# Where a hybrid decoder layer normalises its rows: chunk 0 after the projection instead of before it, chunks 2 and 3 squared ahead of time

## The chip, the cores and the metric

The kernel runs on one core of a Trainium2 chip. The metric is the time of one execution on the device in microseconds (us). TensorE is written PE below, its weight loads PEld, VectorE DVE, ScalarE ACT, GpSimd POOL; SP is SyncE, whose queue issues nearly all transfers.

## The reference

One decoder layer on x of 2048 rows by 1024 columns, float32:

```
hn   = rms_norm(x, g_pre)                 # row * 1/rms(row) * g_pre
proj = hn @ w_in                          # 1024 -> 4096, cut into eight groups of 512
y_rg = rg_lru(conv4(rg_x)) * silu(rg_g)   # gated linear recurrence, 8 heads of 64
y_da = norm((softmax(q1 k1) - lam * softmax(q2 k2)) v) * (1 - l0) * silu(da_g)  # causal, 4 heads
y_xa = softmax(xa_q km) vm * silu(xa_g)   # 4 heads on 256 memory rows, km and vm from rms_norm(mem, g_mem)
out  = x + rms_norm(concat(y_rg, y_da, y_xa) @ w_out, g_post)
```

A row's 1/rms is one number per token, so `(x * r * g) @ w` equals `((x * g) @ w) * r`.

## The kernel before, in words

Each float32 matmul is three float32r matmuls on high and low halves: `mm3` adds hi*hi, lo*hi and hi*lo (L241). A weight piece of 128 by 512 is loaded by `w_load` into one of three raw buffers, and `w_conv` (L327) splits it: ACT casts the high half, POOL or DVE subtracts the low half. The split weights are also stored to memory (`WD`) and loaded back in the second half of the kernel.

Tokens are worked in four chunks of 512. Chunks 0 and 1 go through all 16 pairs of output blocks first, then chunks 2 and 3 in the order `ORDER_B`, then the output projection runs over 16 tiles of 128 rows. A pair has four steps `u`: two chunks by two halves, and a step is 24 matmuls of 512 columns into one of two PSUM banks (`psM`). The evictions `ev_qk`, `ev_v`, `ev_g`, `ev_xa` and `ev_rg` then read the bank.

To feed a chunk, its rows are normalised, transposed on PE in 128 by 128 blocks, scaled by g_pre and split into `hnT` (`transpose_norm`, L293). Chunk 0's rows go through `norm_row` (L264): one half is squared on ACT, one on DVE, a chain of small operations gives 1/rms, and both halves are scaled in place (L275). Chunks 1 to 3 and mem go through `norm_steps` (L277): a square on ACT every `gap` of planned time, then the chain, then all scales at once. In `woven` (L384) the transposes of a chunk stand between the first pair's matmuls, block by block (`kb`).

The order of PE's instructions is that of the program. A planner, `now`, adds up PE's expected time; `spawn` adds a generator that `pump` advances when its due time has come, between matmuls. So attention is woven into the projections: `s_stream` emits the scores (S) of a job, `t_stream` the transposed probabilities times V, `kv_stream` loads keys and values. `room["e"]` counts free score tiles of the pool `pe` (`N_E` = 12), and `kready` and `q2s` hold the planned arrival of keys and the loaded q tiles. A job is a head and a pair of 128-row query blocks. Twelve jobs can be done while chunks 0 and 1 are projected; `next_x` (L919), called at pair 13, waits in the plan for these twelve, then loads the rows of chunks 2 and 3 and spawns their `norm_steps`.

All other engines' queues are ordered by the framework by priority, which is program order unless `high_priority` moves it ahead, and by when its own plan sees operands and buffers ready. So a load can be issued well before its place in the program. Each buffer pool is a set of equal slots (`p2` nine, `p4` seven, `pw` six, `pe` twelve).

Of the kernel before, what the change touches and what calls it, by code (L numbers as in the profile page):

```python
# [57 lines left out]
def hybrid_layer(  # L58
# [66 lines left out]
    ones_r = const.tile([128, 128], F32R, name="ones_r")  # L125
# [16 lines left out]
    def setup():  # L142

        nc.scalar.preload_act_table_set("natural_log_exp_and_others")
        nc.scalar.dma_start(vec, vecs[:, 0:V_CW])
        make_identity(nc, ident)
        nc.gpsimd.memset(cmask, 0.0)
        nc.gpsimd.affine_select(
            out=cmask, in_=cmask, pattern=[[-1, 128]], compare_op=ALU.is_ge,
            fill=NEG, base=0, channel_multiplier=1)  # L150
        nc.vector.memset(epsb, EPS)
        nc.vector.memset(tinyb, 1e-37)
        nc.vector.tensor_scalar(ones_r, ident, 0.0, 1.0, op0=ALU.mult, op1=ALU.add)
# [110 lines left out]
    def norm_row(row):  # L264

        ss = tiny.tile([128, 2], F32, tag="ss1", name="ss1")
        ja, jv = f2("junk", (128, 512)), f2("junk", (128, 512))
        nc.scalar.activation(ja, row[0], AF.Square, accum_out=ss[:, 0:1])
        nc.vector.tensor_tensor_reduce(jv, row[1], row[1], 1.0, 0.0, ALU.mult, ALU.add, ss[:, 1:2])
        r = tiny.tile([128, 1], F32, tag="rs1", name="rs1")  # L270
        with tc.high_priority(offset=2000):
            nc.vector.tensor_add(r, ss[:, 0:1], ss[:, 1:2])
            rsqrt_mean(r, r, D, nc.vector)
            for p in row:
                nc.vector.tensor_scalar_mul(p, p, r)  # L275
# [93 lines left out]
    stored = set()  # L369
    setup()  # L370
# [12 lines left out]

    def woven(c, rows):  # L384

        new_hnT(c)
        os = [ps_m("ip") for _ in range(2)]
        xt = transpose_norm(rows, hnT[c], V_GPRE)
        next(xt)
        next(xt)  # L390
        for kb in range(KB):
            w = wcv[kb // 2]
            for half in range(2):
                cs = slice(half * 128, half * 128 + 128)
# [12 lines left out]
        ready.add(c)  # L407
        return os

# [61 lines left out]

    def ev_qk(h, c, which, o):
        t = f4("qkhl", (128, 2, CH), F32R)
# [16 lines left out]
    def ev_v(hp, c, half, o):  # L490
# [3 lines left out]
        for hh in range(2):  # L494
            nc.scalar.copy(t[:, 0, hh], ov[:, hh])
            nc.vector.tensor_sub(t[:, 1, hh], ov[:, hh], asf(t[:, 0, hh]))
# [5 lines left out]
    def ev_g(hp, c, half, o):  # L502
        t = f2("gs", (128, CH))
# [14 lines left out]
    def ev_xa(h, c, which, o):  # L518
        if which == 0:
# [63 lines left out]
    def ev_rg(b, c, which, o):  # L583
        if which == 0:
# [7 lines left out]
            nc.scalar.copy(xr[:, 3:515], o)  # L592
# [14 lines left out]
        xc, xh = state.pop("xc")  # L607
        gs = f2("rgg", (128, CH))
# [5 lines left out]
    def rg_gates(b, c, xc, xh, gs):  # L614
# [83 lines left out]
    def s_stream(jobs):  # L698

        q2s = {}  # L700

        def q2_load(i):
            if i < 2 * len(jobs) and i not in q2s:
                h, pr = jobs[i // 2]
                if has("qk", h, pr // 4):
                    q2s[i] = load_q2(h, 2 * pr + i % 2)
        due = now[0]
        for ij, (h, pr) in enumerate(jobs):
# [3 lines left out]
            while kready.get((h, pr // 4), 1e9) > now[0]:  # L712
# [119 lines left out]
    def subln(h, pr, A, B):  # L832
        c, j = divmod(pr, 2)
        s = ps_t("ss", (128, 256))
        mm(s, ones_r, B[:, 0, :], True, False)
        mm(s, ones_r, B[:, 1, :], False, True)
# [72 lines left out]
    def start_attention():  # L909
        room["e"] = N_E  # L910
# [6 lines left out]
    xn = {}  # L917

    def next_x():  # L919
# [19 lines left out]
    def start_b():  # L939
# [5 lines left out]
        (2, 0): start_attention,  # L945
        (13, 0): next_x,
# [12 lines left out]

    def load_wout(grp):  # L960
# [6 lines left out]
        for kb in range(4):  # L967
            raw = f4("woraw")
            nc.sync.dma_start(raw, w_out[4 * grp + kb])
# [9 lines left out]
    project((2, 3), 80, ORDER_B, {(0, 0): start_b, (15, 2): last_pair})  # L979
# [118 lines left out]
```

## Time and profile before

| | before |
|---|---|
| time, median of 3 runs | 1467.82 us (1467.02 to 1468.22) |
| the profiled execution | 1467.53 us, span 1465.7 us |
| PE busy, and its mean granted clock | 1412.3 us (96%), 0.994 of full speed |
| DVE, ACT, POOL busy | 898.3, 775.9, 477.3 us |
| transfers | 234.37 MB, mean 160 GB/s |

The span runs from the first to the last instruction. Busy times overlap; an engine's idle time counts only where the chain that sets the end passes through it. PE's matmuls are pipelined, so their busy time can cover short stalls.

### The profile page before, as it was taken

To read this page: it belongs to the slowest core of one execution; us is meant where nothing else is said; L and a number is where in the kernel's file an instruction comes from. 1 tells how busy PE (TensorE), PEld (TensorE's weight loads), DVE (VectorE), ACT (ScalarE), POOL (GpSimd) and SP (SyncE) were. 2 spreads that over 40 slices of the span, in tenths; PEclk is the share of its full clock that TensorE was granted. 3 is DMA by queue.
4 is the path that set the end of the run, shared out by engine and by line. 5 is a ranking of instruction groups with operands and counts; after the bars stand their busy time and mean duration, and the time that the engine had idled before them with its cause. 6 is when DMAs were issued, how large, how long until landed. Compare 5 with 4: busy or idle time off the path is not lost.

```text
span 1465.7 us, 21854 instructions
## 1 busy us (share of the span) xinstructions
PE 1412.3 (96%) x7568; PEld 1199.2 (82%) x7568; DVE 898.3 (61%) x1872; ACT 775.9 (53%) x1900; POOL 477.3 (33%) x568
## 2 busy tenths in 40 slices
PE   5999999999999899999999999999999999999997
PEld 3798889888887678888887898888877888888886
DVE  6531555676644876746547666757678777767222
ACT  6343544666547784745555545555566545554221
POOL 2031333344435632412213222212255333334221
PEclk9999999999999999999999999999999999999999
DMA  8689787745433348356324554232475334322231
GB/s 298 180 263 338 230 240 237 247 143 181 166 119 110 134 163 247 121 173 196 114 97 118 165 177 168 86 113 70 143 251 169 101 135 150 102 76 94 87 122 72
DMA packets 147870, 234.37 MB, mean 160 GB/s; under 512 B 12464, under 2 KB 82224, under 8 KB 147760
## 3 DMA queue, kind: packets, MB, share of 16 engines
q1 hardware_dynamic: 147616, 232.98, 48.8%
q8 instruction: 59, 0.97, 0.3%
q14 instruction: 51, 0.42, 0.1%
q10 hardware_dynamic: 144, 0.01, 0.0%
HBM read 142.76 MB, written 90.18 MB: 159 GB/s over the span
## 4 chain that ended last, share of the span: by engine, by line
PE 73%; DVE 9%; ACT 7%; DMA 4%; POOL 3%; issue 3%; SPq 1%; DVEq 0%; POOLq 0%; ACTq 0%
PE ip L198 36%; PE po L198 16%; PE s L198 7%; PE o L198 6%; PE pt L202 3%; PE xas L198 2%; DVE e L766 1%; DVE nm L740 1%; PE xao L198 1%; DMA q<-QD 1%; DVE xc L600 1%; PE rgo L198 1%; ACT e L742 1%; PE xat L202 1%; POOL e L765 1%
## 5 line engine op out<-in xcount | busy, mean ns | idle before, releaser
L198 PE MATMUL ip<-hnT,wp 128*128 128x512 f32 x2688 | 680.5, 397 | 6.9 <-DVE rgg L610 2.6
L198 PEld LDWEIGHTS ip<-hnT,wp 128*128 128x128 f32 x2688 | 496.0, 190 | 109.8 <-DVE hnT L307 4.5
L742 ACT ACTIVATE e<-s,nm 128x512 f32<-128x512 f32 (+3 forms) x320 | 200.1, 626 | 254.7 <-DVE nm L740 235.8
L740 DVE TENSOR_REDUCE nm<-s 128x1 f32<-128x512 f32 (+3 forms) x320 | 193.4, 605 | 37.4 <-PE s L198 33.1
L198 PE MATMUL po<-wout,yg 128*128 128x512 f32 x768 | 193.4, 393 | 5.0 <-POOL wout L239 2.4
L765 POOL TENSOR_SCALAR e<-e,f 128x512 f32<-128x512 f32 (+3 forms) x160 | 121.3, 773 | 235.5 <-DVE f L761 161.6
L198 PE MATMUL s<-kv,q 128*128 128x512 f32 (+3 forms) x640 | 182.9, 367 | 3.9 <-DMA q<-QD 2.4
L198 PEld LDWEIGHTS po<-wout,yg 128*128 128x128 f32 x768 | 141.1, 188 | 35.4 <-POOL wout L239 4.2
L766 DVE SCALAR_TENSOR_TENSOR e<-e,f 128x512 f32<-128x512 f32 (+3 forms) x160 | 138.0, 887 | 29.9 <-POOL e L765 29.7
L807 DVE TENSOR_TENSOR pthl<-pt,pthl 128x512 fp32r<-128x512 f32 (+1 forms) x144 | 94.5, 656 | 68.0 <-ACT pthl L806 67.5
L198 PE MATMUL o<-pthl,kv 128*128 128x256 f32 (+1 forms) x864 | 134.3, 290 | 1.0 <-DVE pthl L807 0.9
L198 PEld LDWEIGHTS s<-kv,q 128*128 128x128 f32 x640 | 114.5, 189 | 25.1 <-DMA q<-QD 3.0
L239 POOL TENSOR_TENSOR wp<-wraw,wp 128x512 fp32r<-128x512 f32 x67 | 91.1, 1368 | 127.1 <-ACT wp L238 110.8
L198 PEld LDWEIGHTS o<-pthl,kv 128*128 128x128 f32 x864 | 114.1, 189 | 4.5 <-DVE pthl L807 1.8
L806 ACT CAST pthl<-pt 128x512 fp32r<-128x512 f32 (+1 forms) x144 | 80.7, 561 | 55.2 <-PE pt L202 54.5
L239 POOL TENSOR_TENSOR yg<-yraw,yg 128x512 fp32r<-128x512 f32 x48 | 64.2, 1341 | 132.8 <-ACT yg L238 122.4
L198 PE MATMUL ip<-wp,hnT 128*128 128x256 f32 x768 | 99.7, 284 | 1.3 <-POOL wp L239 0.8
L198 PEld LDWEIGHTS ip<-wp,hnT 128*128 128x128 f32 x768 | 95.8, 191 | 3.0 <-POOL wp L239 1.0
L198 PE MATMUL po<-wo,yg 128*128 128x512 f32 x384 | 97.2, 392 | 0.0
L202 PE MATMUL pt<-ident,e 128*128 128x128 f32 x544 | 83.0, 272 | 3.3 <-DVE pthl L807 3.3
L198 PEld LDWEIGHTS po<-wo,yg 128*128 128x128 f32 x384 | 71.0, 188 | 14.3
L202 PEld LDWEIGHTS pt<-ident,e 128*128 128x128 f32 x544 | 66.9, 140 | 18.4 <-DVE pthl L807 3.8
(188 smaller groups left out, 1686.1 us busy)
## 6 DMA issues: line engine op xcount, KB each, us to landing
WD<-wp SPq DMA_DIRECT2D x64, 512.0 KB, 4.7
wp<-WD SPq DMA_DIRECT2D x64, 512.0 KB, 4.3
wraw<-in_w_in_dram SPq DMA_DIRECT2D x64, 256.0 KB, 3.4
q<-QD SPq DMA_DIRECT2D x128, 128.0 KB, 3.7
kv<-KD SPq DMA_DIRECT2D x24, 512.0 KB, 5.9
kv<-VD SPq DMA_DIRECT2D x24, 512.0 KB, 6.2
yraw<-YD SPq DMA_DIRECT2D x48, 256.0 KB, 2.7
QD<-qkhl SPq DMA_DIRECT2D x32, 256.0 KB, 3.5
```

Of the source, the lines that this page charges most:

```text
L198: nc.tensor.matmul(o, w, xx, start=start, stop=stop)
L202: nc.tensor.transpose(o, i, ident)
L239: eng.tensor_sub(lo, raw, asf(hi))
L600: nc.vector.scalar_tensor_tensor(xc[:, 0:CH], xr[:, k:k + CH], vec2[:, cw + k:cw + k + 1], xc[:, 0:CH], op0=ALU.mult, op1=ALU.add)
L740: nc.vector.tensor_reduce(out=nm[:, c, kc:kc + 1], in_=s[:, 0:w], op=ALU.max, axis=AX.X, negate=True)
L742: nc.scalar.activation(e[kc, c][:, 0:w], s[:, 0:w], AF.Exp, bias=nm[:, c, kc:kc + 1], accum_out=l[:, c, kc:kc + 1])
L765: nc.gpsimd.tensor_scalar(e2, e2, f[:, 1, kc:kc + 1], 1.0, op0=ALU.mult, op1=ALU.mult)
L766: nc.vector.scalar_tensor_tensor(e1, e1, f[:, 0, kc:kc + 1], e2, op0=ALU.mult, op1=ALU.add)
L806: nc.scalar.copy(hi[:, 0:n], t[:, 0:n])
L807: nc.vector.tensor_sub(lo[:, 0:n], t[:, 0:n], asf(hi[:, 0:n]))
```

## The change

Chunk 0 is no longer normalised before it is transposed. `norm_row` is gone; `inv_rms`, called in `woven` after block 2, squares chunk 0's eight half-tiles (four on ACT, four on DVE) and leaves 1/rms in `r0`, one column per 128 rows. `spread` transposes each column, broadcast to 128 by 128, on PE, so that every partition of `rB0` holds the 512 numbers, and keeps `rB0` in a `pe` slot. Every result of chunk 0 is multiplied by `rB0` when it leaves PSUM (`normed_out`), and V, whose tokens lie on partitions, by `r0`'s column. x's first halves are loaded before its second halves, with weights 1 and 2 after each; chunk 1 is loaded at block 3, mem after the woven pair. Weight 0 is split on DVE, the other first weights on POOL.

`ahead`, spawned at step (4, 0), loads the rows of chunks 2 and 3 half a tile at a time into one `pe` slot and squares them in place on ACT. `next_x` loads the rows again and spawns `scale_rows`, which scales half a row every `SQ_GAP`. The plan has 11 score tiles, 10 while `ahead` runs.

Besides: `ones_r` is one column that is broadcast; in `rg_gates` the two matmuls on the low half stand behind the four on the high half; `s_stream` waits until 6 planned us after the load of a job's first q tile; the raw rows of w_out's group 2 are asked for at step (15, 3) of the second half.

```diff
-    ones_r = const.tile([128, 128], F32R, name="ones_r")
+    ones_r = const.tile([128, 1], F32R, name="ones_r")
...
-    def norm_row(row):
...
+    def inv_rms(tiles, r):
+        n = len(tiles)
+        ss = tiny.tile([128, 2, n], F32, tag="ss0", name="ss0")
+        for j in range(2):
+            for i, row in enumerate(tiles):
+                junk = f2("junk", (128, 512))
+                if i % 2:
+                    nc.vector.tensor_tensor_reduce(junk, row[j], row[j], 1.0, 0.0, ALU.mult, ALU.add,
+                                                   ss[:, j, i:i + 1])
+                else:
+                    nc.scalar.activation(junk, row[j], AF.Square, accum_out=ss[:, j, i:i + 1])
+        nc.vector.tensor_add(r, ss[:, 0], ss[:, 1])
+        rsqrt_mean(r, r, D, nc.vector)
...
     w_load(0)
-    xr0 = load_rows(x, 4, "xrow")
-    w_load(1, 2)
+    xr0 = [[f2("xrow", (128, 512), pool=pe) for _ in range(2)] for _ in range(4)]
+    for j in range(2):
+        for i in range(4):
+            nc.sync.dma_start(xr0[i][j], x[i * 128:(i + 1) * 128, j * 512:(j + 1) * 512])
+        w_load(1 + j)
+    rB0 = f2("rB0", (128, CH), pool=pe)
     xb = bigt("xrows", (128, 4, 2, 512), F32)
...
-    for i in range(4):
-        nc.sync.dma_start(xb[:, i].rearrange("p a b -> p (a b)"), x[CH + i * 128:CH + (i + 1) * 128, :])
-    mrows = load_rows(mem, 2, "memx")
-    w_conv(0)
-    for row in xr0:
-        norm_row(row)
-    w_conv(1, 2, eng=nc.vector)
+    mrows = []
+    with tc.high_priority(offset=2000):
+        w_conv(0, eng=nc.vector)
+    w_conv(1, 2)
...
             if c == 0:
+                if kb == 2:
+                    with tc.high_priority(offset=1000):
+                        inv_rms(rows, r0)
+                if kb == 6:
+                    spread(r0, 4, rB0)
+                if kb == 3:
+                    for i in range(4):
+                        t0 = CH + i * 128
+                        nc.sync.dma_start(xb[:, i].rearrange("p a b -> p (a b)"), x[t0:t0 + 128, :])
                 if kb in (1, 2, 4, 6):
                     i = {1: 3, 2: 4, 4: 5, 6: 6}[kb]
-                    w_conv(i, eng=nc.vector if i in (3, 5) else nc.gpsimd, pool=pw if i < 6 else p4)
+                    w_conv(i, pool=pw if i < 6 else p4)
...
             w_conv(7, pool=p4)
+            mrows.extend(load_rows(mem, 2, "memx"))
...
+    def spread(r, n, dst):
+        t = ps_t("rb", (128, n * 128))
+        for i in range(n):
+            transpose(t[:, i * 128:(i + 1) * 128], r[:, i:i + 1].to_broadcast([128, 128]))
+        with tc.high_priority(offset=2000):
+            nc.scalar.copy(dst, t)
...
+    def normed_out(o, c):
+        if c:
+            return o
+        n = f2("nrm", (128, CH))
+        nc.vector.tensor_mul(n, o, rB0)
+        return n
...
+        o = normed_out(o, c)
...
+                r = r0[:, 2 * half + i:2 * half + i + 1]
+                nc.scalar.activation(hi, oi, AF.Copy, scale=r)
+                nc.vector.scalar_tensor_tensor(lo, oi, r, asf(hi), op0=ALU.mult, op1=ALU.subtract)
...
-            nc.scalar.copy(xr[:, 3:515], o)
+            if c == 0:
+                nc.vector.tensor_mul(xr[:, 3:515], o, rB0)
+            else:
+                nc.scalar.copy(xr[:, 3:515], o)
...
+        os = [ps_s("rgo") for _ in range(2)]
         for g in range(2):
-            o = ps_s("rgo")
-            mm3(o, state["rgh"][:, b, g, :], state["rgl"][:, b, g, :], xh[:, 0], xh[:, 1], True, True)
+            mm(os[g], state["rgh"][:, b, g, :], xh[:, 0], True, False)
+            mm(os[g], state["rgl"][:, b, g, :], xh[:, 0], False, False)
+        for g in range(2):
+            o = os[g]
+            mm(o, state["rgh"][:, b, g, :], xh[:, 1], False, True)
...
                     q2s[i] = load_q2(h, 2 * pr + i % 2)
+                    landed[i] = now[0] + 6.0
...
-            while kready.get((h, pr // 4), 1e9) > now[0]:
+            while max(kready.get((h, pr // 4), 1e9), landed[2 * ij]) > now[0]:
                 yield 0.5
...
-        room["e"] = N_E
+        room["e"] = N_E - 1
...
+    def ahead():
+        ssx = const.tile([128, 8, 2], F32, name="ssx")
+        while room["e"] < 1:
+            yield 0.4
+        room["e"] -= 1
+        for k in range(16):
+            row = f2("xahead", (128, 512), pool=pe)
+            t0, j = 2 * CH + (k // 2) * 128, k % 2
+            nc.sync.dma_start(row, x[t0:t0 + 128, j * 512:j * 512 + 512])
+            yield 9.0
+            nc.scalar.activation(row, row, AF.Square, accum_out=ssx[:, k // 2, j:j + 1])
+            yield 4.0
+        room["e"] += 1
+        nc.gpsimd.tensor_add(rx, ssx[:, :, 0], ssx[:, :, 1])
+        rsqrt_mean(rx, rx, D)
+
+    def scale_rows(c):
+        for i, row in enumerate(xn[c]):
+            for p in row:
+                nc.vector.tensor_scalar_mul(p, p, rx[:, 4 * (c - 2) + i:4 * (c - 2) + i + 1])
+                yield SQ_GAP
...
-            spawn(norm_steps(xn[c], SQ_GAP), 6.0 if c == 2 else 20.0)
+            spawn(scale_rows(c), 6.0 if c == 2 else 20.0)
...
-            room["e"] += 8
+            room["e"] += 9
...
+        (4, 0): lambda: spawn(ahead()),
...
+    def last_raw():
+        for kb in range(4):
+            wo_load(2, kb)
...
-    project((2, 3), 80, ORDER_B, {(0, 0): start_b, (15, 2): last_pair})
+    project((2, 3), 80, ORDER_B, {(0, 0): start_b, (15, 2): last_pair, (15, 3): last_raw})
```

## Rows read from the trace of the kernel before

**Rows 1.** The page, busy us (share of the span) and instructions of each engine.
```profile
PE 1412.3 (96%) x7568; PEld 1199.2 (82%) x7568; DVE 898.3 (61%) x1872; ACT 775.9 (53%) x1900; POOL 477.3 (33%) x568
```

**Rows 2.** TensorE's waits: line, what for, us in total, times, longest us.
```profile
PE xt L202 <- DVE xrow L275: 14.3, 4, 9.4
...
PE rgo L198 <- POOL xchl L604: 4.0, 5, 1.4
...
PE xas L198 <- DVE xaq L528: 3.4, 3, 1.7
...
PE ip L198 <- DVE rgg L610: 2.6, 2, 1.4
...
PE po L198 <- POOL wout L239: 2.4, 4, 0.7
...
PE s L198 <- DMA q<-QD: 2.4, 1, 2.4
...
PE po L198 <- ACT wout L238: 1.5, 1, 1.5
...
PE ip L198 <- DVE qkhl L476: 1.4, 2, 0.7
```

**Rows 3.** Timeline of the start: start us, busy us, instruction [idle before <-releaser].
```profile
7.39 0.69 DVE L269 CUSTOM_DVE_ANT_0 junk<-xrow 128x512 f32<-128x512 f32 x1
...
15.15 0.88 DVE L275 TENSOR_SCALAR xrow<-xrow,rs 128x512 f32<-128x512 f32 x2
...
16.95 2.93 PE L198 MATMUL ip<-hnT,wp 128*128 128x512 f32 x6
...
47.08 1.03 PE L202 MATMUL xt<-ident,xrows 128*128 128x128 f32 x8
...
50.33 0.60 PE L202 MATMUL xt<-ident,xrows 128*128 128x128 f32 x4
```

**Rows 4.** Windows: us, busy (x) PE PEld DVE ACT POOL, PEclk, DMA share, GB/s.
```profile
480.00:490.00 10.00, 8.08 (x27) 6.19 (x28) 9.58 (x13) 9.44 (x22) 5.04 (x6) 0.83 0.57 205
...
510.00:520.00 10.00, 8.84 (x32) 7.12 (x33) 5.70 (x6) 7.33 (x13) 4.24 (x6) 0.83 0.49 159
```

**Rows 5.** Timeline of the RG-LRU stretch.
```profile
457.28 0.62 ACT L283 ACTIVATE junk<-xrow 128x512 f32<-128x512 f32 x1
...
479.43 7.38 DVE L291 TENSOR_SCALAR xrow<-xrow,rs 128x512 f32<-128x512 f32 x8 [0.94 <-POOL rs L256]
...
480.67 0.73 PE L198 MATMUL rgo<-xchl,rgh 128*128 128x512 f32 x2 [1.40 <-POOL xchl L604]
...
487.45 8.45 PE L198 MATMUL ip<-hnT,wp 128*128 128x512 f32 x36 [1.25 <-DVE rgg L610]
...
511.16 0.73 PE L198 MATMUL rgo<-xchl,rgh 128*128 128x512 f32 x2 [1.16 <-POOL xchl L604]
```

**Rows 6.** Timeline around attention's first scores.
```profile
136.71 1.62 SPq L692 DMA_DIRECT2D q<-QD  x2
...
145.65 0.81 PE L198 MATMUL s<-kv,q 128*128 128x256 f32 x2 [2.38 <-DMA q<-QD]
...
146.30 4.05 PE L198 MATMUL ip<-hnT,wp 128*128 128x512 f32 x10
```

**Rows 7.** Groups: busy us, mean ns of one | idle before, releaser.
```profile
L239 POOL TENSOR_TENSOR wp<-wraw,wp 128x512 fp32r<-128x512 f32 x67 | 91.1, 1368 | 127.1 <-ACT wp L238 110.8 <-DMA kv<-VD 15.9
...
L505 DVE TENSOR_TENSOR gs<-ip,gs 128x512 f32<-128x512 f32 x16 | 11.0, 689 | 27.3 <-ACT gs L262 27.0
```

**Rows 8.** ScalarE's waits, one row.
```profile
ACT wp L238 <- DMA wraw<-in_w_in_dram: 13.9, 11, 2.5
```

**Rows 9.** Timeline: end of attention's first part, and w_out.
```profile
413.71 0.40 PE L198 MATMUL ss<-sq,ones_r 128*128 128x256 f32 x2
...
1083.92 10.68 SPq L969 DMA_DIRECT2D woraw<-in_w_out_dram  x5
...
1092.35 0.73 PE L198 MATMUL po<-wout,yg 128*128 128x512 f32 x2 [1.52 <-ACT wout L238]
```

More of the change, by code (lines that the diff above doesn't have):

```diff
@@ L152, in setup @@
         nc.vector.memset(tinyb, 1e-37)
-        nc.vector.tensor_scalar(ones_r, ident, 0.0, 1.0, op0=ALU.mult, op1=ALU.add)
+        nc.vector.tensor_scalar(ones_r, ident[:, 0:1], 0.0, 1.0, op0=ALU.mult, op1=ALU.add)
     def setup2():
@@ L262, in sigmoid @@
         nc.scalar.activation(o, o, AF.Exp, scale=-1.0)
-    def norm_row(row):
[L266 to L275, printed above, removed]
+    def inv_rms(tiles, r):
[11 more added lines that the diff above has]
+        rsqrt_mean(r, r, D, nc.vector)
     def norm_steps(tiles, gap, eng=nc.gpsimd, prio=2000):
@@ L369, in hybrid_layer @@
     stored = set()
+    r0 = const.tile([128, 4], F32, name="r0")
     setup()
     w_load(0)
-    xr0 = load_rows(x, 4, "xrow")
-    w_load(1, 2)
+    xr0 = [[f2("xrow", (128, 512), pool=pe) for _ in range(2)] for _ in range(4)]
[4 more added lines that the diff above has]
+    rB0 = f2("rB0", (128, CH), pool=pe)
     xb = bigt("xrows", (128, 4, 2, 512), F32)
     xr1 = [[xb[:, i, j, :] for j in range(2)] for i in range(4)]
-    for i in range(4):
-        nc.sync.dma_start(xb[:, i].rearrange("p a b -> p (a b)"), x[CH + i * 128:CH + (i + 1) * 128, :])
-    mrows = load_rows(mem, 2, "memx")
-    w_conv(0)
-    for row in xr0:
-        norm_row(row)
-    w_conv(1, 2, eng=nc.vector)
+    mrows = []
+    with tc.high_priority(offset=2000):
+        w_conv(0, eng=nc.vector)
+    w_conv(1, 2)
     def woven(c, rows):
@@ L493, in ev_v @@
         ov = o.rearrange("p (t h d) -> p h t d", t=2, h=2)
-        for hh in range(2):
-            nc.scalar.copy(t[:, 0, hh], ov[:, hh])
-            nc.vector.tensor_sub(t[:, 1, hh], ov[:, hh], asf(t[:, 0, hh]))
+        for i in range(2):
+            if c:
+                hi, lo, oi = t[:, 0, i], t[:, 1, i], ov[:, i]
+                nc.scalar.copy(hi, oi)
+                nc.vector.tensor_sub(lo, oi, asf(hi))
+            else:
+                hi, lo, oi = t[:, 0, :, i], t[:, 1, :, i], ov[:, :, i]
+                r = r0[:, 2 * half + i:2 * half + i + 1]
+                nc.scalar.activation(hi, oi, AF.Copy, scale=r)
+                nc.vector.scalar_tensor_tensor(lo, oi, r, asf(hi), op0=ALU.mult, op1=ALU.subtract)
         def st():
@@ L502, in ev_g @@
     def ev_g(hp, c, half, o):
+        o = normed_out(o, c)
         t = f2("gs", (128, CH))
@@ L518, in ev_xa @@
     def ev_xa(h, c, which, o):
+        o = normed_out(o, c)
         if which == 0:
@@ L591, in ev_rg @@
                 nc.gpsimd.tensor_copy(xr[:, 0:3], halo[:, b, :])
-            nc.scalar.copy(xr[:, 3:515], o)
+            if c == 0:
+                nc.vector.tensor_mul(xr[:, 3:515], o, rB0)
+            else:
+                nc.scalar.copy(xr[:, 3:515], o)
             if c < NCH - 1:
@@ L607, in ev_rg @@
         xc, xh = state.pop("xc")
+        o = normed_out(o, c)
         gs = f2("rgg", (128, CH))
@@ L698, in s_stream @@
     def s_stream(jobs):
-        q2s = {}
+        q2s, landed = {}, {}
         def q2_load(i):
@@ L834, in subln @@
         s = ps_t("ss", (128, 256))
-        mm(s, ones_r, B[:, 0, :], True, False)
-        mm(s, ones_r, B[:, 1, :], False, True)
+        ones = ones_r.to_broadcast([128, 128])
+        mm(s, ones, B[:, 0, :], True, False)
+        mm(s, ones, B[:, 1, :], False, True)
         r = A[:, 1, :]
@@ L917, in hybrid_layer @@
     xn = {}
+    rx = const.tile([128, 8], F32, name="rx")
+    def ahead():
[18 more added lines that the diff above has]
+                yield SQ_GAP
     def next_x():
@@ L957, in y_granule, with wo_load @@
         return g
+    woraw = {}
+    def wo_load(grp, kb):
+        if (grp, kb) not in woraw:
+            raw = woraw[grp, kb] = f4("woraw", pool=pw if grp == 2 and kb == 3 else p4)
+            nc.sync.dma_start(raw, w_out[4 * grp + kb])
+        return woraw[grp, kb]
     def load_wout(grp):
@@ L967, in load_wout @@
         for kb in range(4):
-            raw = f4("woraw")
-            nc.sync.dma_start(raw, w_out[4 * grp + kb])
+            raw = wo_load(grp, kb)
             for j in range(2):
```

## The prediction

> **What bounds the kernel now.** I read the page's busy line first, then TensorE's waits, then the start and the stretches that the waits point at. TensorE has a matmul in flight 96% of the span, and no engine but its own weight loads passes 61% [rows 1]. Busy time of pipelined matmuls flatters the engine, so I don't look for time inside it: what can be won is its idle time, 1465.7 - 1412.3 = 53.4 us, and what is lost while its clock is granted below full speed. The largest part of the idle time lies before the first projection matmul at 16.95: TensorE waited 14.3 us for scaled rows of x [rows 2, 3]. The last few us follow the last matmul and are not touched. The rest is in short waits: 4.0 us for the low half of the conv output in the RG-LRU gates, 3.4 for the cross-attention q, 2.6 for `rgg`, 2.4 for a q load, 3.9 (2.4 plus 1.5) for w_out [rows 2].
>
> The PE order is written by hand and kept; the other queues are ordered by priority, and a load can be issued before its place in the program. So each edit is priced as a wait on TensorE that it shortens or makes; work added on another engine costs nothing by itself.
>
> **First chunk.** Before, TensorE can't transpose a row until it is squared, its 1/rms computed and its halves scaled. The last row's two scales start at 15.15 and take 0.88, so its first half is ready near 15.6; from there to the first projection matmul it is 16.95 - 15.6 = 1.35 us [rows 3]. After the change raw rows are transposed, and only four half-tiles, one per row, follow weight 0 in the queue. Before, the queue held weight 0 and then row 0's and row 1's halves; the fourth x tile was in use at 7.39 [rows 3]. All these tiles are of one size, so the four first halves are there by about 7.4, and the first projection matmul starts at 7.4 + 1.35 = 8.75: **8.2 us earlier**.
>
> What is late next? A woven block is six matmuls of 0.235 (36 in 8.45 us [rows 5]) and four transposes of 0.6 in all [rows 3]: 2.0 us. The second halves are needed at block 4, near 17. They are the tenth tile in the queue; five were in by 7.39, so ten are in by 14.8 even at the pace of the slow start. r0 is computed on ACT and VectorE from then and is needed after block 6, near 23. `spread` adds four PE transposes, 0.6; its ACT copy stands before the first two evictions. Weights 1 to 7 now take their low half on GpSimd, 1.37 us each [rows 7]; one is needed every two blocks (4 us), and matmuls hide it. Without that cover each would cost its 1.37. Moved DMAs: chunk 1's four loads of 512 KB and mem's four of 256 KB stand behind weights 3 to 6 in SP's program order, no longer ahead of them. That helps those weights and makes chunk 1 later, while its first transposes come some 8 us before 47.08 [rows 3]. If a chunk-1 row or a weight is late, TensorE waits for it; the nearest row is ACT's longest wait for a weight, 2.5 us [rows 8]. Bounds for this give-back are 0 and 2.5; I take 1.0, as most weights arrived in time before. Net **8.2 - 0.6 - 1.0 = 6.6**, bounds 5.1 and 7.6.
>
> **Evictions of chunk 0.** 28 tiles get a VectorE multiply by `rB0`; for four of them it stands in for an ACT copy. A multiply of this shape that reads PSUM takes 0.69 [rows 7]: 28 x 0.69 = 19 us, on an engine that is free for 1465.7 - 898.3 = 567 us [rows 1]. V tiles keep their count of operations. The multiply frees the PSUM bank before a sigmoid instead of after it and before the two q/k passes, so it can save the 1.4 us of waits on `qkhl` [rows 2]; I take 0.7. Against it, the cross-attention q of chunk 0 becomes multiply, cast, subtract, 0.69 later for four tiles. `xas` waited for such tiles three times already, so the price is 0 to 4 x 0.69 = 2.8; I take 1.0. Queued behind the new VectorE work are the maxima of s, which release exp; they have high priority.
>
> **Squares moved to attention's first part.** Near 450 to 540 TensorE runs the RG-LRU pairs without attention beside them. The squares for chunk 2 begin at 457.28 on ACT, chunk 3's follow; then eight scales at high priority hold VectorE from 479.43 for 7.38 us. `rgg` waits in that queue, and TensorE waits 1.25 for its PSUM bank [rows 5]. Over 480:490 and again over 510:520 the clock is granted at 0.83 on average [rows 4]; between the levels of 2.4 and 1.2 GHz that loses 0.17 x 10 = 1.7 us each time. Before the first dip TensorE had waited 1.40 for `xchl`, around the second 1.16 [rows 5]. The change takes 16 squares out of this stretch and spaces the scales. I credit the two `rgg` waits, 2.6 [rows 2], and one dip, 1.7: 4.3.
>
> In the gates two more matmuls, 0.47 us, now come ahead of the first use of the low half, so each of the five waits (4.0 in all [rows 2]) can lose up to 0.47, 2.3 together; I take 1.4, as some are shorter. I deduct 0.3 for the multiplies here. **5.4**; bounds 1.4 (the gates alone) and 10 (2.6 + 4.0 + both dips).
>
> What this costs: 16 more loads of 256 KB, 4 MB, on SP's queue, and 16 squares in place on ACT, 0.62 each and an accumulator read [rows 5], in a part where ACT has room (53% overall [rows 1]). If a row is late, ACT's queue stops with exp behind it and the three s banks fill. 16 x 2.5 = 40 us of ACT idle is the far bound [rows 8]; TensorE feels only what outlasts three banks. I take 1.0, and 0 to 5 for the range. `ones_r` and r0 as broadcast operands: the trace has no such load. A weight load has a mean of 1199.2/7568 = 0.16 us [rows 1]; the 64 of `ones_r`, twice as long and uncovered, would be 10 us. I take 0, since loads overlap matmuls; as many columns are loaded as before, which gives no reason for a gain.
>
> Here a rule of the Trainium skill speaks against the change ("SBUF — State Buffer", Who interferes with whom): GpSimd and VectorE share a port pair, so that a VectorE instruction with two SBUF inputs, or in a two-port mode, and a GpSimd instruction that reads SBUF block each other. The trace agrees with it: two scales took 0.88 at the start, eight in the burst 7.38, or 0.92 each, beside GpSimd subtracts [rows 3, 5]. By the rule the splits handed to GpSimd and the 16 scales can cost each other 16 x 0.48 = 8 us; by the rows the scales are off TensorE's path once they are spaced, and the sum stays as it is.
>
> **Waiting for q.** `landed` is checked for index 2*ij alone, the first q tile of a job. TensorE's one wait, 2.4 us at 145.65, is on a tile issued at 136.71, with the first job's second block [rows 6]. So I credit **0**; bound: 2.4 plus ten slow matmuls behind it, 4.05 - 10 x 0.235 = 1.7, together 4.1.
>
> **w_out early.** The raw rows were issued from 1083.92, and TensorE was let go at 1092.35 [rows 9]. `last_raw` asks for them one step (24 matmuls, 5.6 us) sooner, but three of the four still need a buffer of the same pool. I take **2.0** of the 3.9 us, bounds 0 and 3.9.
>
> **One or two fewer score tiles.** A finished job of pr = 3 holds 4 while the next one's first block uses 4; that is 8, and 10 are left. I take 0.
>
> **Sum.** 6.6 + 0.7 - 1.0 + 5.4 - 1.0 + 0 + 2.0 = 12.7. The profiled execution took 1467.53, 1.83 more than its span and 0.29 below the median of the runs: 1467.5 - 12.7 = 1454.8, about **1455**.
>
> **Rivals.**
> - *Head alone* (0.20): new VectorE and ACT waits eat all but the 6.6: 1461. For it: VectorE is 96% and ACT 94% busy in 480:490 [rows 4]. Against it: what fills VectorE there is the burst that is spread.
> - *More than forecast* (0.12): the second dip (1.7), the q wait (4.1) and the rest of the w_out and gate waits (4) go too: 1445. For it: the idle time is there. Against it: nothing asks for that q sooner.
> - *Given back at once* (0.06): chunk 1 or the weights bound the first 60 us (-4), and the multiplies eat the rest: 1465 to 1470.
> - *Slower* (0.07): score tiles run out. Attention's first part ended at 413.71; the squares, spawned 6 us after a drain that wants twelve jobs done, began at 457.28 [rows 5, 9]: a margin of 451 - 414 = 37 us. If each of 12 jobs lost two s steps of 3.08 planned us, that is 74, 37 beyond the margin, in which TensorE has attention's work alone; half idle, it loses 18 and more: 1455 + 18 = 1473. It decides from 37 us on. Against it: the count of 8 above.
>
> **Chances and range.** The forecast, 1448 to 1459, holds 0.55. A measurement here tells a change from none at about 0.2%, 2.9 us. Faster: 0.55 + 0.20 + 0.12 = 0.87; same 0.06; slower 0.07. For 8 in 10 the range reaches from 1445, the case where most goes, to the head alone with 2 us of new waits: 1445 to 1463.
>
> **What would show it.** First `ip` matmul between 8 and 10 and no wait on `xrow`; woven transposes of chunk 1 some 7 us before 47.08; no scale burst, no `rgg` wait and at most one slow-clock stretch between 440 and 540; the first job's q wait still there; less waiting for w_out. Wrong if TensorE waits for `wp` or `xrows` in the first 50 us, if ACT waits for `xahead`, or if the clock dips elsewhere.

## The result: 0.6% slower, and the profile after

| | before | after |
|---|---|---|
| median of 5 runs | 1468.22 us | 1477.46 us (1475.11 to 1479.26) |
| ratio, 95% interval | | 1.0057 (1.0039 to 1.0075) |
| the profiled execution, its span | 1467.53, 1465.7 us | 1478.85, 1477.1 us |

The changed kernel is some 8 us slower (0.57%, by the ratio); the forecast was 12.7 us faster. TensorE's busy line of the page after answers to [rows 1]:

```profile
PE 1419.8 (96%) x7572; PEld 1205.5 (82%) x7572; DVE 901.9 (61%) x1871; ACT 773.5 (52%) x1889; POOL 475.8 (32%) x565
```

Idle time went from 53.4 to 57.3 us, and busy time rose by 7.5. Only 0.4 of that is new work (four transposes of 0.109); some 5 are matmuls at the lower clock, as the table below has three more such stretches of 3.4 us. TensorE's waits after, to set against [rows 2] (line, what for, us in total, times, longest):

```profile
PE xt L202 <- DMA xrow<-in_x_dram: 6.2, 4, 4.3
...
PE s L198 <- DMA q<-QD: 3.7, 1, 3.7
PE ip L198 <- DVE rgg L658: 3.6, 2, 2.4
PE xt L202 <- DVE hnT L309: 3.6, 2, 1.9
PE xas L198 <- DVE xaq L572: 3.0, 5, 1.1
PE kv L198 <- DVE wp L239: 3.0, 1, 3.0
PE s L198 <- ACT e L795: 2.8, 2, 2.0
PE xas L198 <- ACT xaq L571: 2.7, 2, 2.2
...
PE rgo L198 <- POOL xchl L651: 2.4, 2, 1.2
...
PE xt L202 <- DVE xrows L293: 1.9, 2, 1.4
PE rgo L198 <- DVE xchl L650: 1.5, 2, 0.8
...
PE ip L198 <- DVE qkhl L510: 0.7, 1, 0.7
```

The wait for scaled rows of chunk 0, 14.3 us, has shrunk to 6.2 for the raw rows. Small waits took its place, the longest 3.0 us, beside the q wait that was there before. Waits for w_out are gone; the wait for `rgg` is not, it went from 2.6 to 3.6.

Waits alone don't tell the sum, as the clock goes with them. So I counted each stretch: every matmul or transpose is charged the usual distance from its start to the next one's in these traces (0.228 us for 512 columns, 0.175 for 384, 0.1195 for 256, 0.109 for a transpose); what the stretch took beyond that is lost, by waiting or by the clock. "spells" are the stretches in which the clock was granted at 1.2 GHz, after the start and before the end, and their us. "First rows" ends at the first projection matmul, "mem" is the memory branch up to pair 2, where attention begins; pairs 8 to 11 hold the cross-attention, 12 to 15 the RG-LRU. Each row is one profiled execution; executions of one kernel differ by some us, so a number counts here where several kernels agree on it.

```
us lost        first  chunk chunk  mem  pairs pairs pairs second out-   sum  spells
               rows     0     1         2-7   8-11  12-15 half   put
before          16.1   6.2   1.6   1.4   7.8   4.7  13.3  13.5   9.7   74.2  4, 13.6
after            9.9   4.2   5.5   5.7  10.4  11.8  13.1  16.8   7.4   84.8  7, 23.8
e6_headonly      9.8   4.2   5.5   6.2  10.1   7.5  20.2  13.7  11.6   88.9  6, 30.6
e7_nohead       15.7   6.9   1.6   1.6  12.1   8.6   6.5  14.6   6.7   74.1  3, 10.2
e12_nogates     15.8   7.1   1.6   1.5  12.0   8.5   8.1  12.2   7.4   74.2  3, 10.2
e9_norgmul       9.9   4.2   4.1   4.9  10.1  10.8   7.8  15.0   7.2   74.0  3, 13.6
e4_noxamul      10.3   4.2   4.1   5.8   9.2  11.2  13.6  15.4   6.8   80.6  6, 20.4
e3_noahead      11.0   3.8   5.6   5.1   7.3   8.1  21.0  15.1   7.1   84.0  6, 23.8
e10_cures       11.1   3.7   1.6   8.8   3.6  12.7  13.9  18.2   6.8   80.4  7, 27.2
e13_cures2      11.6   3.2   2.0   0.3   5.7  11.9  13.1  16.6   6.6   71.0  3, 10.2
e14_gatesonly   16.4   6.7   1.6   1.3   8.0   4.6  16.1  16.8  11.0   82.5  5, 20.4
e15_afternog    10.4   3.1   5.7   5.0   8.6  12.2  11.5  13.6   6.7   76.7  4, 13.6
e16_best        11.3   4.0   2.0   0.3   8.1  15.3  12.2  13.7   7.1   74.0  6, 23.8
e18_rxdve       11.1   3.2   2.1   0.3   7.7  11.2  12.1  13.9   6.7   68.3  5, 17.0
```

Read the first two rows against each other: 8.2 us won by the end of chunk 0, and given back to the last tenth by the time attention begins (3.9 in chunk 1, 4.3 in the memory branch); 2.6 and 7.1 lost in pairs 2 to 11, nothing won in the RG-LRU pairs 12 to 15, 3.3 lost in the second half, 2.3 won at the output.

**Where the head start went.** These are rows of the timeline after, from the start on (start us, busy us, instruction, idle before it and its releaser):

```profile
8.22 0.62 ACT L238 CAST wp<-wraw 128x512 fp32r<-128x512 f32 x1 [1.29 <-DMA wraw<-in_w_in_dram]
...
9.44 0.63 ACT L275 ACTIVATE junk<-xrow 128x512 f32<-128x512 f32 x1 [0.61 <-DMA xrow<-in_x_dram]
...
10.07 0.67 ACT L308 ACTIVATE hnT<-xt,vec 128x512 fp32r<-128x512 f32 x1
...
10.79 2.94 PE L198 MATMUL ip<-hnT,wp 128*128 128x512 f32 x6 [1.88 <-ACT hnT L308]
...
36.05 0.61 ACT L285 ACTIVATE junk<-xrows 128x512 f32<-128x512 f32 x1
...
40.06 1.26 ACT L308 ACTIVATE hnT<-xt,vec 128x512 fp32r<-128x512 f32 x2 [3.30 <-PE xt L202]
...
41.73 0.21 ACT L251 ACTIVATE rs<-rsv 128x4 f32<-128x4 f32 x1
...
48.26 0.33 PE L202 MATMUL xt<-ident,xrows 128*128 128x128 f32 x1 [1.44 <-DVE xrows L293]
...
88.06 0.41 DVE L488 TENSOR_TENSOR kml<-kv,kmh 128x256 fp32r<-128x256 f32 x1
88.39 0.68 DVE L239 TENSOR_TENSOR wp<-wraw,wp 128x512 fp32r<-128x512 f32 x1
...
89.12 8.50 PE L198 MATMUL kv<-wp,memT 128*128 128x256 f32 x54 [2.98 <-DVE wp L239]
```

Three times the same picture, a queue that stands in order behind something late. At 8.22 ScalarE casts weight 1, for which it had to wait, then squares a half-tile for which it had to wait, and only then makes the first `hnT`: the first projection matmul starts at 10.79, not at 8.75. At 36 to 41 the last square of chunk 1 is done, but `rs` needs ScalarE again (L251), which stands behind two `hnT` that wait 3.30 for TensorE itself; the scales come late and TensorE waits at 48.26. At 88 VectorE has just ended a chain of some 30 small operations on the lambda and LRU constants (80.14 to 88.14), and the weight that TensorE needs at 89 comes behind it. Behind waits like these the clock falls. Windows of the changed kernel (us, busy of PE, PEld, DVE, ACT, POOL, then PEclk, DMA share, GB/s):

```profile
48.80:52.20 3.40, 3.15 (x9) 2.47 (x10) 2.52 (x6) 0.77 (x2) 0.00 (x0) 0.51 0.83 231
89.80:93.20 3.40, 3.40 (x18) 3.40 (x17) 1.12 (x2) 1.41 (x3) 0.59 (x1) 0.50 0.82 301
397.00:400.40 3.40, 3.19 (x13) 2.90 (x14) 2.84 (x5) 0.46 (x1) 2.04 (x5) 0.50 0.69 262
468.70:472.10 3.40, 3.40 (x9) 2.63 (x9) 2.50 (x4) 0.78 (x2) 1.59 (x3) 0.50 0.15 63
```

At half the clock 3.4 us do 1.7 us of work, so each of these four waits cost 1.7 on top of its length, while TensorE shows as busy.

### The profile page after: what moved, and what is told of

Read it like the earlier page. It is cut to its first block, busy times and chain, and to the rows that moved or that the text cites. A ratio compares the mean times of both kernels' runs of the same rounds, so it can differ in the third digit from the quotient of the medians.

```text
span 1477.1 us, 21856 instructions
## 1 busy us (share of the span) xinstructions
PE 1419.8 (96%) x7572; PEld 1205.5 (82%) x7572; DVE 901.9 (61%) x1871; ACT 773.5 (52%) x1889; POOL 475.8 (32%) x565
## 5 line engine op out<-in xcount | busy, mean ns | idle before, releaser
L239 POOL TENSOR_TENSOR wp<-wraw,wp 128x512 fp32r<-128x512 f32 x70 | 95.0, 1364 | 120.8 <-ACT wp L238 115.7
L198 PEld LDWEIGHTS po<-wo,yg 128*128 128x128 f32 x384 | 71.4, 189 | 14.3
```

The source lines that it names most:

```text
L198: nc.tensor.matmul(o, w, xx, start=start, stop=stop)
L239: eng.tensor_sub(lo, raw, asf(hi))
```

## The experiments

Each ratio is to runs of the kernel before on the same chip, so it compares better than the medians.

```
kernel          median us  ratio to before (95%)
e1_setup         1479.93   1.0065 (1.0046 to 1.0084)
e2_x1            1477.62   1.0058 (1.0040 to 1.0075)
e3_noahead       1478.33   1.0060 (1.0045 to 1.0075)
e4_noxamul       1474.35   1.0033 (1.0017 to 1.0049)
e5_x1early       1485.95   1.0088 (1.0058 to 1.0118)
e6_headonly      1479.71   1.0064 (1.0045 to 1.0083)
e7_nohead        1470.08   0.9997 (0.9983 to 1.0011)
e8_noland        1477.75   1.0055 (1.0033 to 1.0076)
e9_norgmul       1470.87   0.9990 (0.9977 to 1.0003)
e10_cures        1472.49   1.0001 (0.9985 to 1.0016)
e11_aheadfix     1473.40   1.0002 (0.9985 to 1.0020)
e12_nogates      1467.10   0.9971 (0.9955 to 0.9986)
e13_cures2       1471.27   1.0008 (0.9996 to 1.0020)
e14_gatesonly    1475.82   1.0032 (1.0019 to 1.0046)
e15_afternog     1473.77   1.0015 (1.0001 to 1.0028)
e16_best         1467.60   0.9976 (0.9964 to 0.9988)
e17_curesonly    1472.76   0.9997 (0.9981 to 1.0013)
e18_rxdve        1462.69   0.9948 (0.9931 to 0.9965)
```

**The change in two parts.** `e6_headonly` is the kernel before with chunk 0's part alone, `e7_nohead` with all the rest.

> The kernel before with the first chunk's part alone (raw rows transposed, 1/rms multiplied into the results, the loads moved); squares, gates, q wait and w_out as before. Forecast's steps: 6.6 + 0.7 - 1.0 = 6.3 less than before, 1462. Theory 'the head start is eaten by what comes late next, and the multiplies cost the cross-attention q some 3 us': nothing is left at 101 us, and 1469 to 1472 at the end.

> The kernel before with everything but the first chunk's part: squares moved, gates reordered, q wait, w_out, ones_r. Forecast's steps: 5.4 - 1.0 + 2.0 = 6.4 less than before, 1462. Theory 'the squares in ScalarE's queue hold up the cross-attention q by 4, the gates gain nothing, w_out gives 2.6, and the rest is small waits from another order': 1468 to 1473.

The first chunk's part carries the whole loss, and more than I expected of it; the rest makes no difference. The forecast had some 6 us of gain for each half: it was off by about 16 us in the first and 6 in the second. The table places them: without the head the RG-LRU pairs lose 6.5, with it alone 20.2, with both 13.1. The squares' gain is real, and chunk 0's part eats it.

**Chunk 0's multiplies.** One leaves them out of the cross-attention, one out of the RG-LRU pairs.

```diff
     def ev_xa(h, c, which, o):
-        o = normed_out(o, c)          # e4_noxamul
...
-            if c == 0:                # e9_norgmul
-                nc.vector.tensor_mul(xr[:, 3:515], o, rB0)
-            else:
-                nc.scalar.copy(xr[:, 3:515], o)
+            nc.scalar.copy(xr[:, 3:515], o)
...
         xc, xh = state.pop("xc")
-        o = normed_out(o, c)
```

> The changed kernel without the multiply by rB0 in the cross-attention evictions of chunk 0 (that part of the scaling is left out). Theory 'the multiply on the q path costs TensorE': the waits for xaq at 291 and 313 us (0.9 and 1.07) shrink, 2 to 3 us less: 1474.5 to 1475.5. Rival 'the multiplies are hidden': 1477, within 1 us.

> The changed kernel without the two multiplies by rB0 in each RG-LRU pair of chunk 0 (ScalarE copies the conv input again, the gate is taken unscaled: that part of the scaling is left out). Theory 'the multiplies lengthen the VectorE chain of the RG-LRU pairs': the stretch from the first RG-LRU pair to the end of the first half loses 6.5 as without the first chunk's part, instead of 13.1; 1471 us. Forecast's step: these multiplies cost 0.3, 1477.

By the ratios they take 0.24% and 0.67% less than the changed kernel. The first time is near the one its theory had, but 0.24% is just what two such ratios can tell apart, and the trace doesn't bear the theory out: pairs 8 to 11 lose 11.2 in place of 11.8. The waits for `xaq` shrink from 5.1 to 3.4, and a new one of 1.6 takes their place (at 286.94, for the bank that `xag` reads: ScalarE had stopped 3.79 us for `xahead` ahead of its sigmoid). The multiply had let go of that bank earlier. The second theory held: pairs 12 to 15 lose 7.8 in place of 13.1, and without these eight multiplies the whole loss against the kernel before is gone. The traced execution, the fastest of its twelve, loses 10.8 less than the changed kernel's, 5.3 of it here. TensorE's waits in the RG-LRU pairs, first with chunk 0's part alone, then in the changed kernel, then without these multiplies:

```profile
PE rgo L198 <- POOL xchl L651: 5.9, 4, 2.5
PE ip L198 <- DVE rgg L658: 3.2, 2, 1.8
PE rgo L198 <- DVE xchl L650: 2.9, 2, 1.5
...
```

```profile
PE ip L198 <- DVE rgg L658: 3.6, 2, 2.4
PE rgo L198 <- POOL xchl L651: 2.4, 2, 1.2
PE xt L202 <- DVE hnT L309: 1.7, 1, 1.7
PE rgo L198 <- DVE xchl L650: 1.5, 2, 0.8
```

```profile
PE ip L198 <- DVE rgg L658: 3.6, 2, 2.4
PE rgo L198 <- POOL xchl L651: 1.6, 2, 0.8
```

With the burst of scales still in VectorE's queue (first fence) `xchl` costs 8.8 us; the multiply stands at the head of the chain xr, conv, `xchl` and in its queue. Without the multiplies VectorE's part of `xchl` is no longer waited for. `rgg` is waited for in each of the three, burst or none.

**What eats the head start.** Cures for the late chains, singly and together, on the changed kernel.

```diff
-    store(setup2, 52.0)
+    store(setup2, 28.0)               # e1_setup, e10_cures; 80.0 in e13_cures2
...
-                if kb == 3:
-                    for i in range(4):
...
+    for i in range(4):                # chunk 1, after weight 2: e2_x1, e5_x1early, e10_cures, e13_cures2
...
     def prep_x1():
-        yield 9.0
+        yield 2.0                     # e5_x1early, e10_cures, e13_cures2
         yield from norm_steps(xr1, 1.3, prio=0)
-        yield 8.0
+        yield 0.5                     # e13_cures2, with mem's loads at kb == 4
...
-                w_load(i + 3)
+                for k in range(i + 1, i + 6):   # e10_cures, e13_cures2: five memory weights
+                    if k not in wseen and (k <= i + 3 or MEM0 + 3 <= k < MEM0 + 16):
+                        w_load(k)     # every other one in a slot of pe
```

> One number of the changed kernel is altered: the lambda and LRU constants (two small loads, some 30 small serial VectorE operations of 7.9 us) are emitted at planned time 28 instead of 52, so that they stand in VectorE's queue where the kernel before had them, ahead of mem's transposes and not in the middle of the memory branch. Theory 'the head start is real and is eaten by what comes late next': TensorE's 2.98 us wait for a weight's low half at 89 us and the half-clock spell behind it go, the memory branch loses about 1.1 us as before instead of 5.5, and the kernel takes 1473 us (4.4 less). Rival 'the memory weights themselves arrive late, as their loads are issued behind stores': the wait stays, and the time stays at 1477.

> The changed kernel with chunk 1's four loads issued right after weight 2 again, ahead of weights 3 to 6. Theory 'eaten by what comes late next': chunk 1's squares start some 8 us earlier, its scales are done before its transposes, TensorE's waits of 1.44 and 0.46 for xrows at 48 to 49 us and the half-clock spell go; the stretch from the woven chunk 1 to the end of its second pair loses 1.6 instead of 5.5, and the kernel takes 1473.5 us (3.9 less). Rival 'weights take its place': weights 3 to 6 land later, TensorE waits for wp within the first 40 us, and the first 60 us take as long as in the changed kernel: 1477.

> The changed kernel with chunk 1's loads right after weight 2 and its squares emitted 7 us of planned time sooner (2.0 instead of 9.0). The loads alone changed nothing, as the squares kept their place in ScalarE's queue, behind activations that wait for TensorE. Theory 'a queue place behind TensorE-bound work': now rs is done before the woven chunk 1 begins, the wait for xrows and the half-clock spell at 48 us go, that stretch loses 1.6 instead of 5.5, mem's rows follow sooner too, and the kernel takes 1472 to 1474 us. Rival 'squares ahead of the first transposes' evictions cost as much': TensorE waits for hnT in the first woven chunk instead, and the time stays at 1477.

> The changed kernel with three cures for what came late in its first 115 us: chunk 1's loads after weight 2 and its squares 7 us of planned time sooner; the lambda and LRU constants at planned time 28 instead of 52; five instead of three memory weights in flight, in buffers that are free there. Theory 'the head start is eaten by three queues that had run ahead while TensorE waited for its first rows': with all three cured, TensorE is 5 to 8 us ahead of the changed kernel where attention's first pair begins (95 us instead of 101.3), and at 114. Rival 'something else holds the memory branch': it begins at 99 to 101 us again. Of the total time less is asked, as the order of all that follows is planned anew: 1471 to 1480.

> The three cures, with two more: mem's loads and squares come sooner as well (loads at the first chunk's fifth block, squares right after chunk 1's), and the lambda and LRU constants wait until planned time 80, after the memory branch. Before, with three cures, the woven chunk 1 lost 1.6 and the memory branch 0.1, but mem's rows, next in the same queue, held TensorE 5.5 us at 63. Theory 'the head start was eaten by queues one after the other': now attention's first pair begins near 93 to 95 us instead of 101.3, and the kernel takes 1465 to 1470. Rival 'a floor under the first 100 us, as of the weights' transfers': 99 to 101 again.

One cure alone gained nothing, so what I had expected of single chains was wrong. With the constants earlier the wait at 89 went, but their VectorE chain then held mem's rows (1.4 at 65). Earlier loads for chunk 1 changed nothing: the squares, not the loads, are behind TensorE-bound work. With the squares earlier, chunk 1 lost 2.2 instead of 5.5, and TensorE waited later for a weight (3.4); its total rose to 1486, which this chain doesn't explain. Three cures together brought chunk 1 and the weights in order, and mem's rows, next in the same queues, cost 5.5 (squared at 57 to 60, their scales on VectorE beside the constants). Only all five hold it. Their run's timeline around attention's first pair:

```profile
85.72 7.48 PE L198 MATMUL kv<-wp,memT 128*128 128x256 f32 x61
93.05 13.12 PE L198 MATMUL ip<-wp,hnT 128*128 128x256 f32 x108
```

The pair begins at 93.05, no wait before it; in the changed kernel at 101.26. So there is no floor under the first 100 us. The total says less: with three cures, where the pair began at 101.01, it is 1.0001 of the kernel before, with all five 1.0008, so no gain at the end is shown for the 8 us held at this point. The control gives the kernel before the same cures:

> Control: the kernel before with the same cures and without the change (five memory weights in flight, squares of chunk 1 and of mem sooner, constants after the memory branch). Theory 'the queues ran ahead while TensorE waited, so nothing is late there before the change': attention's first pair begins at 99 to 101 us as before, and the time is that of the kernel before within 0.2%. Rival 'the cures are worth 8 us by themselves': 1462.

0.9997: there they are worth nothing to the total. One part of that expectation failed: the first pair begins at 105.17, not at 99 to 101, after longer waits for `qkhl` (2.6) and a weight (1.3), and the time is won back later. The rival is out all the same. In the kernel before, TensorE waits 0.6 for a weight between 18 and 101 us and not at all for `xrows` or mem's rows. What is late after the change had been early enough before; as I read it, because TensorE stood still for its first 17 us while the other queues ran on.

**The squares.** `e3_noahead` puts `norm_steps` back in place of `ahead` and `scale_rows`; `e11_aheadfix` gives the loads more planned time and spreads the rsqrt, in the kernel without the head.

> The changed kernel without the 16 extra loads and squares: the rows of chunks 2 and 3 are squared and scaled in one go again, after attention's first part. Theory 'the squares in ScalarE's queue hold up the cross-attention q': the wait of 2.2 us for xaq at 397 us and its half-clock spell go, the stretch of pairs 8 to 11 loses 6 to 7 instead of 11.8 us, and the RG-LRU stretch loses 13 as in both kernels: 1472 us. Rival 'the forecast's step': the burst of scales is back in the RG-LRU stretch and costs it 4.3 us, so that the two cancel or the kernel gets slower: 1477 or more.

> Everything but the first chunk's part, as before, with the extra loads given 11 us of planned time instead of 9 and the rsqrt of the 8 row sums spread out: 8 us of planned time between GpSimd's part and ScalarE's, so that ScalarE doesn't stop for it ahead of the cross-attention's q. Theory 'the price of the squares is ScalarE's queue stopping': the wait of 2.0 us for xaq at 396 and the half-clock spell behind it go, 3.7 us less than without the fix, 1466, which beats the kernel before. Rival 'another wait takes its place': 1470.

Without the squares pairs 8 to 11 lose 8.1 and not 11.8, and pairs 12 to 15 lose 21.0 and not 13.1; the time is the same within the interval, as pairs 2 to 7 lose 3.1 and the second half 1.7 less. The burst has its price, as the forecast had it, and the squares have theirs. ScalarE's and TensorE's timeline of the changed kernel shows what the squares cost:

```profile
393.70 0.63 ACT L986 ACTIVATE xahead<-xahead 128x512 f32<-128x512 f32 x1 [2.06 <-DMA xahead<-in_x_dram]
...
396.17 0.21 ACT L251 ACTIVATE rx<-rsv 128x8 f32<-128x8 f32 x1 [1.74 <-POOL rsv L250]
396.28 0.57 ACT L571 CAST xaq<-ip 128x512 fp32r<-128x512 f32 x1
...
396.90 0.52 PE L198 MATMUL xas<-kmh,xaq 128*128 128x256 f32 x1 [2.21 <-ACT xaq L571]
```

The cast of `xaq` stands behind a square that waits for its row and an rsqrt of 8 numbers per partition that waits for GpSimd. The Trainium skill says that the queues of ScalarE, VectorE and GpSimd are strict FIFO ("PSUM — Partial Sum Buffer", Engine vs sequencer instructions); these rows agree. The fix missed it: the wait for `xaq` stayed, 2.0, as ScalarE stood 3.17 us ahead of its Ln, the first step of that rsqrt, GpSimd having a scaling (1.57) and a weight split (1.72) ahead of the 8 sums.

**The gates and the q check.** `e12_nogates` is `e7_nohead` with the old order of the gates' matmuls, `e14_gatesonly` the kernel before with the new one, `e15_afternog` the changed kernel with the old. `e8_noland` is the changed kernel without `landed`.

> Everything but the first chunk's part and but the new order of the gates' matmuls. Forecast's step: the order of the gates is worth 1.4 us: 1471.5. Rival 'the gates order frees TensorE from xchl and keeps the clock up': xchl waits come back from 1.8 to 4 us with one half-clock spell, 1473 to 1475. Other rival 'it is worth nothing': 1470.

> The kernel before with the new order of the gates' matmuls alone. Forecast's step: 1.4 less, by shorter waits for xchl. Theory 'both gates hold two of the three s banks at once, and the pairs of the second half that run beside attention wait for it': about 1.6 less in the RG-LRU stretch, 4 more between 540 and 690 us, so 2 to 3 slower than before.

> The changed kernel with the old order of the gates' matmuls. Theory as above: the waits at 554 (for hnT) and 690 us (for pthl) go, 4 us, the RG-LRU stretch loses 1 to 2 more: 1474 to 1475. Forecast's step: 1.4 slower than the changed kernel.

> The changed kernel without the landed check on q. Forecast's step: the check is worth nothing, 1477. Theory 'the check gives up score steps in attention's first part and so shifts other work onto waits': the waits of pairs 8 to 11 shrink, 1473 to 1475.

In all three pairs of kernels the new order is the slower one: by 0.26%, 0.32% and 0.42%, and in a fourth pair, `e13_cures2` with it and `e16_best` without, by 0.32%. The RG-LRU pairs gain 1.6 (8.1 to 6.5) in one pair of kernels and lose 0.9 to 2.8 in the others; the second half loses 2.4 to 3.3 in all. TensorE's waits between 543 and 700 us with the new order alone:

```profile
PE s L198 <- ACT e L746: 2.7, 2, 1.8
PE xt L202 <- DVE hnT L307: 1.4, 1, 1.4
PE o L198 <- DVE pthl L811: 0.5, 1, 0.5
```

There, in the kernel before, only 1.0 for `e` and 0.3 for `xchl`. A score waits for exp to let go of its bank; that both gates now hold two of the three s banks fits it, but is argued, as no run gave the gates other banks. Without `landed` the q wait is 4.2 (3.7 with it): the check is worth nothing, as forecast.

**A version that beats both.** `e16_best` is `e13_cures2` with the old gates; `e18_rxdve` also moves the 8 row sums to VectorE.

```diff
-        nc.gpsimd.tensor_add(rx, ssx[:, :, 0], ssx[:, :, 1])
-        rsqrt_mean(rx, rx, D)
+        nc.vector.tensor_add(rx, ssx[:, :, 0], ssx[:, :, 1])
+        rsqrt_mean(rx, rx, D, nc.vector)
```

> The changed kernel with all five cures and the old order of the gates' matmuls. If the two findings add up: 1471 less 4 to 6 for the gates, 1465 to 1467, faster than the kernel before by 0.2 to 0.4%. If the gates' order cost only by chance of the planning: 1471, no difference.

> The fastest combination so far with the chain of the 8 row sums on VectorE instead of GpSimd. In the run that only gave it more planned time, ScalarE's Ln still stood 3.17 us ahead of the cross-attention's q, since GpSimd did a scaling of 1.57 and a weight split of 1.72 first. Now ScalarE's order changes in one place alone: the cast of xaq stands ahead of that Ln. Theory 'ScalarE's queue stopped by a small result': the wait of 2 us for xaq near 390 and the half-clock spell behind it go, 3.7 us less in pairs 8 to 11, 1464. Rival 'the q was late for another reason': no change, 1467.6.

Both times came as expected: 0.24% and 0.52% faster than the kernel before. But `e12_nogates`, without chunk 0's part, is faster by 0.29%: even with the five cures that part is worth nothing at the end, and no run put the row sums on VectorE without it. From `e16_best` to `e18_rxdve` ScalarE's order changes in one place and TensorE's in none, so it is the cleanest evidence here that ScalarE's queue was a price of the squares: 0.28%, and 15.3 to 11.2 in pairs 8 to 11. Part of that fall is the single execution: `e16_best` has a spell of double length there, and the changed kernel, with the same wait and one of 3.4 us, loses 11.8. Most of the wait came back (2.24 to 1.67), for `xaq`'s low half on VectorE, but without the spell at the lower clock that had followed it:

```profile
386.70 0.39 PE L198 MATMUL xas<-kmh,xaq 128*128 128x256 f32 x1 [1.67 <-DVE xaq L576]
```

## Why the prediction was wrong

- **First chunk, 8.2 - 0.6 - 1.0.** The raw halves were there when forecast (the fourth is transposed at 7.59), but the first projection matmul started at 10.79: 6.2 won and not 8.2, as weight 1 and a square stood ahead of `hnT` in ScalarE's queue. Chunk 0 then lost 2.0 less than before, which I hadn't credited, so that the gain at its end, 8.2, meets the forecast by luck. The failed step is the give-back, "I take 1.0, as most weights arrived in time before", bounds 0 and 2.5. It was 8.2, all of the gain: chunk 1's rows, mem's rows and the memory weights had been on time only because TensorE started late. The far bound should have been the whole head start. TensorE itself did not wait for weights 1 to 7.
- **Evictions, 28 multiplies for +0.7 - 1.0 - 0.3.** The 0.7 came: the wait for `qkhl` went from 1.4 to 0.7. The 1.0 for the cross-attention stays unsure: 2.8 with chunk 0's part alone (4.7 to 7.5), 0.6 by leaving these multiplies out. The second failed step is the 0.3 for the RG-LRU pairs: 5.3 without these multiplies there, and 3.4 to 6.9 between kernels with and without chunk 0's part (11.5 and 8.1, 20.2 and 13.3). I had set the work against an engine that is free for 567 us. Even in this stretch VectorE is free 40% of the time after the change (first row below); what the multiply lengthens is the chain that TensorE waits for.
- **Squares moved, 4.3.** Right in size by itself: 13.3 to 8.1, 5.2, with the old gates. But that is luck in part, as it came not by the `rgg` waits (2.6 to 2.2, and 3.6 with the new gates) but by the clock: the granted mean over these pairs was 0.97 before, with both dips of [rows 4] where I had credited one; in `e12_nogates` it is 1.00. In the changed kernel the multiplies take the gain back. The windows of pairs 12 to 15 in the changed kernel, the kernel before and `e12_nogates`:

```profile
430.30:549.90 119.60, 110.24 (x500) 88.72 (x498) 71.89 (x92) 71.20 (x127) 52.28 (x59) 0.99 0.37 127
```

```profile
419.90:539.70 119.80, 112.12 (x498) 89.59 (x497) 79.08 (x102) 83.67 (x168) 58.13 (x72) 0.97 0.38 129
```

```profile
428.70:543.30 114.60, 108.17 (x498) 87.54 (x497) 70.33 (x86) 74.40 (x132) 53.34 (x60) 1.00 0.40 134
```

- **Gates, 1.4.** Wrong in sign: shorter waits at the gates in one kernel, but waits for scores in the second half in all.
- **`ahead`, 1.0 of 0 to 5.** The place was right, ScalarE's queue stopped for 10.1 us in all, the size was 3.7 to 3.9 in pairs 8 to 11. What the queue held up in the changed kernel was the cast of `xaq`, not exp. Pairs 2 to 7 lose 4.2 more in the kernels without the head. In `e7_nohead` these are small waits: 1.7 in place of 0.5 for a weight at 105, which comes ahead of the first extra load (154), 1.2 in place of 0.4 for `gs`, 1.1 more for `pthl` and `sq`; why the weight is late there stays open.
- **w_out, 2.0; q, 0.** 2.3 to 3.0 and 0: right. `ones_r`, 0: right, its 64 weight loads took 188 ns each before, from a full tile, and after, from one broadcast column:

```profile
L198 PEld LDWEIGHTS ss<-sq,ones_r 128*128 128x128 f32 x64 | 11.4, 188 | 2.1
```

```profile
L198 PEld LDWEIGHTS ss<-sq,ones_r 128*128 128x128 f32 x64 | 11.5, 188 | 3.6 <-ACT sq L879 1.0 <-POOL sq L880 0.6
```

- **The rivals.** "Given back at once" had the first mechanism, by chunk 1, and both its prices were too low; "slower" named score tiles, which nothing here shows. The signs of being wrong that the prediction names all came: a wait for `xrows` at 48.26, ScalarE's waits for `xahead`, dips of the clock elsewhere.

## What to carry to other kernels

When the engine that sets the time is let go earlier, everything that had run ahead of it in the meantime becomes late next: list the queues by their lead at that point, and take the whole gain as the bound of the give-back until each has been moved too. Whether a lead that is held early still counts at the end is a question of its own. Price an added operation in the stretch where it runs, by the chain it lengthens and by what stands behind it in its queue, not by its engine's free time over the span. A small result that one engine must wait for, put into another's in-order queue, can be as dear as a large one.

## What I hadn't expected of the hardware

After waits of 1.4 to 3.0 us (ending at 48.26, 89.12, 396.90 and 468.40) the clock stood at 1.2 GHz within a microsecond, which made each of them about 1.7 us dearer; a wait of 2.0 that ended at 684.30 in the same execution was not followed by such a spell.

```profile
468.40 10.06 PE L198 MATMUL ip<-hnT,wp 128*128 128x512 f32 x36 [2.41 <-DVE rgg L658]
...
684.30 0.73 PE L198 MATMUL s<-kv,q 128*128 128x512 f32 x2 [1.98 <-ACT e L795]
```

The mean granted clock differs between executions of one kernel, and the time mostly with it: the twelve of `e13_cures2` ran from 1465.21 us at 0.995 to 1474.57 at 0.990.

The mean of 0.92 us that the prediction gives for a scale in the burst hides two sorts: of the eight in [rows 5] four took 0.47 us, and the four that ran while GpSimd had a subtract or a multiply took 1.47 to 1.55.
